# A two-layer trunk of four parallel mixers: layer 0 opens tile by tile of the channels over all eight PSUM banks

## The chip, the cores and the metric

One Trainium2 chip, one core of it. The metric is the device time of one execution in microseconds. The engines: TensorE (PE) multiplies matrices, VectorE (DVE), ScalarE (ACT) and GpSimd (POOL) do the elementwise work, SyncE (SP) issues most transfers. Each engine takes its instructions in the order in which the program gives them.

## What is computed

Two layers on 256 tokens of 1024 channels, all in float32. Each layer norms x, scales and shifts it by the conditioning c, multiplies it by one wide input matrix (7124 columns), sends the columns through four mixers, merges these by gates, projects, adds, and then runs a squared-ReLU MLP. Cut:

```python
for l in range(DEPTH):
    cmod = (c_act @ ada_w[l] + ada_b[l])[:, None, :]
    sh1, sc1, g1, sh2, sc2, g2 = jnp.split(cmod, 6, axis=-1)
    h = _rmsnorm(x, norm_mix_g[l]) * (1.0 + sc1) + sh1
    z = h @ w_in[l]
    za, zb, zc, zd, zg = _split(z, [A_COLS, B_COLS, C_COLS, D_COLS, G_COLS])
    ya = _conv_branch(za, ...)         # gate and value, convolution of 31 taps
    yb = _sparse_attn_branch(zb, ...)  # top 64 keys of an indexer, attention
    yc = _gla_branch(zc, ...)          # gated linear recurrence
    yd = _hgrn2_branch(zd, ...)        # gated linear recurrence
    gates = jax.nn.sigmoid(zg).reshape(B_, S_, N_BRANCH, D_)
    merged = jnp.sum(jnp.einsum('bsnw,nwd->bsnd', ys, w_branch_out[l]) * gates, axis=2)
    x = x + g1 * (merged @ w_o[l])
    h = _rmsnorm(x, norm_mlp_g[l]) * (1.0 + sc2) + sh2
    x = x + g2 * (jnp.square(jax.nn.relu(h @ mlp_w1[l])) @ mlp_w2[l])
return _rmsnorm(x, final_g)
```

## The kernel before

A product is made of float32r matmuls: each operand is split into a high and a low part, and three products (high by high, high by low, low by high) are accumulated in PSUM (`mm3`). A weight slab of up to 128 x 1024 is loaded by SP (`do_load`, line 412, pool `raw` of 5 places, and 8 more places for the first conditioning slabs), and split by ScalarE (high part `wh`) and VectorE (low part `wl`) in `do_split` (429). A conditioning slab isn't split: VectorE multiplies it by c and sums it along the row into one column (`use`, 650; a "sum" below).

The order of all instructions is written by the planner in the kernel. `items` are the steps of TensorE's main stream, each with the slabs it needs; `run` (453) goes through them, loads ahead as places come free, and splits ahead as far as `LOOK` (6500 ns of planned work) unless an item says otherwise. Smaller work lies in chains (generators): B0 and B1 (attention of the two token tiles), A (convolution), C and D (recurrences). `weave` (196) puts steps of chains between the matmuls where the planner's clocks (`note`, durations in `_Meter`) say that their inputs are there, and `drain` (208) emits a chain to its end, and of the others every step that would start earlier by those clocks, with a handicap of 300 ns plus the chain's `PRIO` (88: B 300, D 400, C 500, A 1000). In `_Meter` an affine_select of GpSimd is priced at 330 ns plus 10 ns a row of its innermost dimension, a memset or copy of 256 elements at 245 ns.

PSUM has eight banks: four (`mm`, taken by `mm_take`) serve the main stream, four are the mixers' working banks (`b2`, two pairs, 1035); in the opening of layer 0 the latter four hold the transposed x (`accs`).

The opening of layer 0 (`start`, 1564, and `layer`, 1596): SP loads the small inputs, c on all partitions (`crow`), two conditioning slabs and then x. `norm_first` (785) norms x, transposes it into the four `accs` banks, and, as each channel tile's scale and shift have been summed up, makes hT, the high and low part of that tile of h, from there. `early(k)` (1618) multiplies channel tile k by branch B's 724 columns (slabs b0, b1; tokens on partitions, four `mm` banks, 12 matmuls of 362 columns). The conditioning slabs come two of the scale and two of the shift at a time. `mask_consts` (990) makes seven masks for the recurrences on GpSimd in this stage, and `other_consts` (865) the tables of angles, bounds, selectors. After branch B, `change` (1666) opens the mixers' pools and spawns B0 and B1, and chunks of columns follow with the columns on partitions (`chan_chunk`, 561): ag and av (the convolution's gate and value), df and dq (D's forget and query factors), 48 matmuls of 256 columns each. Then di (with the tokens on partitions, 48 matmuls of 512 columns), cqk, cv, and the gates and projections of B, D, C, A in this order (`merge_items`, 1491), each of which drains its own chain first. The conditioning slabs for later parts are spread between these (`spread`, 379). In a level of `linear` (1283) two small products are followed by VectorE work and by a predicated copy that reads that level's mask.

Of the kernel before, what the change touches and what calls it, by code (L numbers as in the profile page):

```python
# [17 lines left out]
try:  # L18
# [15 lines left out]
P = 128  # L34
S = 256
# [38 lines left out]
# pieces of the input projection: columns, and how many k tiles a slab holds  # L74
WIN = {"b0": ([(512, 874)], 2), "b1": ([(874, 1220), (1988, 2004)], 2), "df": ([(2004, 2260)], 4),
       "dq": ([(2260, 2516)], 4), "di": ([(2516, 3028)], 2), "cqk": ([(1220, 1476)], 4),
       "cv": ([(1476, 1988)], 2), "av": ([(0, 256)], 4), "ag": ([(256, 512)], 4)}
for _i in range(8):
    WIN[f"g{_i}"] = ([(COL_G + 512 * _i, COL_G + 512 * _i + 512)], 2)
WIN_AT = {}  # L80
_off = 0
for _c, (_cols, _per) in WIN.items():
    _n = sum(b - a for a, b in _cols)
    WIN_AT[_c] = (_off, _n, _per)
    _off += _n * D
# [10 lines left out]
class Flow:  # L96
    """Emission order: a stream of weight slabs for the tensor engine, with chains of smaller work
    woven in between where a rough model of the engines says that their inputs are there."""
# [109 lines left out]
    def drain(self, ch, until=None):  # L208
        """emits a chain to its end (or until something holds), and what else can go on meanwhile"""
# [68 lines left out]
class _Pool:  # L278
    """a pool whose tiles are short-lived: the model knows when their places are free"""
# [15 lines left out]
class Slab:  # L295
    """A piece of a weight matrix: loaded, and split into two float32r parts when it says so."""
# [10 lines left out]
class Item:  # L307
    """A step of the tensor engine's main stream: the slabs it uses, what emits it, what comes before."""
# [8 lines left out]
def trunk_kernel(ctx, tc, x, c, cT, pos, chan, ada_w, ada_t, w_in, mlp_w1, gla_gate_w,  # L317
# [1668 lines left out]
```

## Time and profile before

| what | before |
| --- | --- |
| device time, median of 3 runs | 941.81 us (940.19 to 946.4) |
| span of the profiled execution | 943.6 us |
| TensorE busy in it | 897.3 us (95%) |
| VectorE busy | 713.9 us (76%) |
| ScalarE busy | 478.9 us (51%) |
| GpSimd busy | 110.4 us (12%) |
| read from memory | 194.97 MB, 208 GB/s over the span |

A busy engine is one that has an instruction in flight. A matmul's listed duration includes its way through the array, so neighbouring matmuls overlap; what one costs in a row of them is the distance between their starts. The granted clock is the share of full speed at which TensorE was allowed to run: 1.00 is 2.4 GHz, and 0.50 is 1.2 GHz.

### The profile page before, as it was taken

To read this page: it belongs to the slowest core of one execution; us is meant where nothing else is said; L and a number is where in the kernel's file an instruction comes from. 1 tells how busy PE (TensorE), PEld (TensorE's weight loads), DVE (VectorE), ACT (ScalarE), POOL (GpSimd) and SP (SyncE) were. 2 spreads that over 40 slices of the span, in tenths; PEclk is the share of its full clock that TensorE was granted. 3 is DMA by queue.
4 is the path that set the end of the run, shared out by engine and by line. 5 is a ranking of instruction groups with operands and counts; after the bars stand their busy time and mean duration, and the time that the engine had idled before them with its cause. 6 is when DMAs were issued, how large, how long until landed. Compare 5 with 4: busy or idle time off the path is not lost. (4 is left out here: it accounts for less than half of the span.)

```text
span 943.6 us, 14391 instructions
## 1 busy us (share of the span) xinstructions
PE 897.3 (95%) x5320; PEld 753.0 (80%) x5320; DVE 713.9 (76%) x1204; ACT 478.9 (51%) x787; POOL 110.4 (12%) x158
## 2 busy tenths in 40 slices
PE   1699999999999999999999999999999999999996
PEld 1699766767778899998978887777777889999995
DVE  7989788787767878888776988887876784555553
ACT  6474754324454544444575567333455564544451
POOL 6800010101000001111110001021000001111110
PEclk9899999999999999999999999999999999999998
DMA  8878545465644598999954554445655456666641
GB/s 315 307 253 284 188 152 179 163 194 179 230 144 158 194 312 322 316 316 315 323 192 174 168 180 155 137 151 158 223 166 172 153 183 221 225 210 216 219 158 46
DMA packets 55558, 196.96 MB, mean 209 GB/s; under 512 B 6432, under 2 KB 6848, under 8 KB 55488
## 3 DMA queue, kind: packets, MB, share of 16 engines
q1 hardware_dynamic: 55488, 196.04, 61.8%
q8 instruction: 42, 0.69, 0.3%
q14 instruction: 28, 0.23, 0.1%
HBM read 194.97 MB, written 1.05 MB: 208 GB/s over the span
## 5 line engine op out<-in xcount | busy, mean ns | idle before, releaser
L273 DVE TENSOR_TENSOR wl<-raw,wh 128x1024 fp32r<-128x1024 f32 (+1 forms) x276 | 329.3, 1219 | 64.7 <-ACT wh L273 63.5
L273 ACT ACTIVATE wh<-raw 128x1024 fp32r<-128x1024 f32 (+1 forms) x276 | 277.6, 1040 | 129.9 <-DMA raw<-in_mlp_w 73.5
L273 PE MATMUL mm<-wh,hTh 128*128 128x512 f32 (+1 forms) x384 | 155.0, 404 | 8.5 <-ACT wh L273 5.1
L273 PE MATMUL mm<-wl,hTh 128*128 128x512 f32 (+1 forms) x384 | 148.1, 386 | 5.5 <-DVE wl L273 5.4
L273 PE MATMUL mm<-wh,hTl 128*128 128x512 f32 (+1 forms) x384 | 147.7, 385 | 0.0
L273 PE MATMUL mm<-h2h,wl 128*128 128x256 f32 x416 | 117.2, 282 | 0.0
L273 PE MATMUL mm<-h2l,wh 128*128 128x256 f32 x416 | 117.2, 282 | 0.0
L273 PE MATMUL mm<-h2h,wh 128*128 128x256 f32 x416 | 117.1, 282 | 0.0
L273 PEld LDWEIGHTS mm<-wh,hTh 128*128 128x128 f32 x384 | 73.2, 191 | 37.2 <-issue 11.9
L273 PE MATMUL acc<-wh,uH 128*128 128x512 f32 x256 | 101.7, 397 | 0.0
L273 PE MATMUL acc<-wl,uH 128*128 128x512 f32 x256 | 101.2, 395 | 0.5 <-DVE wl L273 0.5
L273 PE MATMUL acc<-wh,uL 128*128 128x512 f32 x256 | 101.1, 395 | 0.1
L273 DVE SCALAR_TENSOR_TENSOR raw<-raw,crow 128x1024 f32<-128x1024 f32 x72 | 90.8, 1269 | 3.0 <-DMA raw<-in_ada_t 2.7
L273 PEld LDWEIGHTS mm<-wl,hTh 128*128 128x128 f32 x384 | 73.4, 191 | 17.0 <-DVE wl L273 6.6
L273 PEld LDWEIGHTS mm<-wh,hTl 128*128 128x128 f32 x384 | 73.3, 191 | 13.8 <-DVE hTl L273 0.3
L273 PEld LDWEIGHTS mm<-h2h,wh 128*128 128x128 f32 x416 | 78.3, 188 | 1.0
L273 PEld LDWEIGHTS mm<-h2l,wh 128*128 128x128 f32 x416 | 78.3, 188 | 1.1
L273 PEld LDWEIGHTS mm<-h2h,wl 128*128 128x128 f32 x416 | 78.3, 188 | 0.1
L273 PEld LDWEIGHTS acc<-wh,uL 128*128 128x128 f32 x256 | 48.2, 188 | 11.5 <-DVE uL L273 0.5
L273 PEld LDWEIGHTS acc<-wl,uH 128*128 128x128 f32 x256 | 48.2, 188 | 11.0 <-DVE wl L273 1.1
L273 PEld LDWEIGHTS acc<-wh,uH 128*128 128x128 f32 x256 | 48.2, 188 | 9.7
L273 DVE SCALAR_TENSOR_TENSOR ca<-U,chp,ca 128x256 f32<-128x256 f32 x120 | 53.3, 493 | 0.0
(532 smaller groups left out, 1452.7 us busy)
## 6 DMA issues: line engine op xcount, KB each, us to landing
raw<-in_mlp_w SPq DMA_DIRECT2D x128, 512.0 KB, 5.1
raw<-in_w_in SPq DMA_DIRECT2D x100, 512.0 KB, 4.2
raw<-in_ada_t SPq DMA_DIRECT2D x72, 512.0 KB, 5.5
raw<-in_ada_w SPq DMA_DIRECT2D x24, 512.0 KB, 4.2
raw<-in_w_branch_out SPq DMA_DIRECT2D x16, 512.0 KB, 4.2
raw<-in_w_o SPq DMA_DIRECT2D x16, 512.0 KB, 4.2
raw<-in_w_in SPq DMA_DIRECT2D x16, 362.0 KB, 4.3
x<-in_x SPq DMA_DIRECT2D x2, 512.0 KB, 7.6
```

What stands on the lines that cost most here:

```text
L273: return fn(*args, **kw)
```

## The change

- Layer 0's input columns are packed anew: per channel tile one slab o0 of branch B's 724 columns and one slab o1 of 1024 columns (ag, av, df, dq). Layer 1 keeps its packing.
- The opening runs channel tile by channel tile: load and sum the tile's scale and shift, split o0 and o1, make the tile of h, and multiply it by both slabs at once: 12 matmuls of 362 columns into the four `mm` banks, 24 of 256 columns into the four `accs` banks (two results of 256 columns to a bank). All eight banks hold running sums until tile 7 is done.
- x is loaded first, on SP's queue; c, positions and the per-channel parameters are loaded from ScalarE's queue. c is no longer loaded on all partitions, but spread by eight matmuls and two copies. x is normed (VectorE multiplies, ScalarE did before), transposed, and copied from PSUM to SBUF once (`xT`), so that the banks are free.
- After tile 7 one item, `opened`, spawns the masks, empties all eight banks, opens the mixers' pools, spawns B0, B1, A and D, and drains the masks. Then comes di, as before.
- The masks' scratch is bf16 in a place of its own. The small rows (gw, ngc, ngd) are loaded in `opened`. The sines are computed after tile 0.

```diff
-WIN = {"b0": ([(512, 874)], 2), "b1": ([(874, 1220), (1988, 2004)], 2), "df": ([(2004, 2260)], 4),
-       "dq": ([(2260, 2516)], 4), "di": ([(2516, 3028)], 2), "cqk": ([(1220, 1476)], 4),
-       "cv": ([(1476, 1988)], 2), "av": ([(0, 256)], 4), "ag": ([(256, 512)], 4)}
...
+    _REST[f"g{_i}"] = ([(COL_G + 512 * _i, COL_G + 512 * _i + 512)], 2)
+
+WIN = [{"o0": ([(512, 1220), (1988, 2004)], 1), "o1": ([(256, 512), (0, 256), (2004, 2516)], 1), **_REST},
+       {"b0": ([(512, 874)], 2), "b1": ([(874, 1220), (1988, 2004)], 2), "df": ([(2004, 2260)], 4),
+        "dq": ([(2260, 2516)], 4), "av": ([(0, 256)], 4), "ag": ([(256, 512)], 4), **_REST}]
...
+            junk = xTp.tile([P, D], BF16, name="junk1", tag="junk1")
+            A.activation(junk, xt[t], AF.Square, scale=1.0 / 32.0, accum_out=ss[:, 0:1])
+            G.tensor_scalar(ss[:, 0:1], ss[:, 0:1], EPS, None, op0=OP.add)
+            rs.append(rstd_of(ss[:, 0:1], 1))
+        for t in range(NT):
...
+                V.tensor_scalar(y, xt[t][:, c * 512:(c + 1) * 512], rs[t], None, op0=OP.mult)
+                pss[t, c] = bank(t, c)
                 for kk in range(4):
-                    T.transpose(pss[t, c][:, kk, :], y[:, kk * P:(kk + 1) * P], ident)
...
+    def tile_first(k, scale, shift, h):
+
+        scale.finish_on_act(k)
+        shift.finish_on_act(k)
+        tm = work.tile([P, 512], F32, name="hf", tag="t512", bufs=5)[:, 0:S]
+        A.activation(tm, state["xT"][:, k, :], AF.Identity, scale=scale.col[:, k:k + 1],
+                     bias=shift.col[:, k:k + 1])
+        A.activation(h[0][:, k, :], tm, AF.Copy)
+        V.tensor_tensor(h[1][:, k, :], tm, h[0][:, k, :].bitcast(F32), op=OP.subtract)
...
+        def angles():
+            for r in range(2):
+                A.activation(sin2[:, :, r, :], ang, AF.Sin)
+                A.activation(cos2[:, :, r, :], ang2, AF.Sin)
+        state["angles"] = angles
...
     def mask_consts():
-        while "rms" not in state:
-            fl.ctx.blocked = True
-            fl.ctx.t = fl.clock["pe"] + 300.0
-            yield
-        fl.ctx.blocked = False
         masks = consts.tile([P, 7, S], U8, name="masks")
-        mks = zp.tile([P, NT * 704 + 64], F32, name="mks", tag="Z")
+        mks = consts.tile([P, 2, S], BF16, name="mks")
...
         for lv in range(7):
-            yield
+            yield "pool"
...
+            mk = mks[:, lv % 2, :]
+            G.memset(mk, 1.0)
+            mv = mk.rearrange("p (r b i) -> p r b i", r=4, i=m)
...
-            G.tensor_copy(masks[:, lv, :], mk32)
...
+            G.tensor_copy(masks[:, lv, :], mk)
...
-        nc.sync.dma_start(ccol, cT)
-        nc.sync.dma_start(crow, bass.AP(tensor=c.tensor, offset=c.offset, ap=[[0, P], [1, D]]))
-        sp["t"] = 2000.0
...
+        nonlocal xTp
+        xTp = state["ctx"].enter_context(tc.tile_pool(name="xTp", bufs=1, side="right"))
+        nc.scalar.dma_start(ccol, cT)
+        nc.scalar.dma_start(posi, pos)
+        nc.scalar.dma_start(chp, chan)
+        for t in range(NT):
+            nc.sync.dma_start(xt[t], x[t * P:(t + 1) * P, :])
...
+        for _ in range(4):
             do_load(pos_of["load"])
...
+        A.activation(cg, ccol, AF.Sigmoid)
+        V.tensor_tensor(cs, ccol, cg, op=OP.mult)
+        G.tensor_copy(cb, cs[:, :, None].to_broadcast([P, KD, 32]))
+        pcs = mm_take(2)
+        for c in range(2):
+            for j in range(4):
+                k = 4 * c + j
+                T.matmul(pcs[c][:, j * P:(j + 1) * P], cs[:, k:k + 1].to_broadcast([P, P]), ident,
+                         start=True, stop=True)
+        other_consts()
+        V.tensor_copy(crow[:, 0:512], pcs[0])
+        pool = state["ctxp"].enter_context(tc.tile_pool(name="accs", bufs=1, space=PSUM))
+        state["bank"] = lambda t, c: pool.tile([P, 512], F32, name="accs", tag=f"accs{t}{c}")
+        state["xps"] = rows_first(state["bank"])
+        A.activation(crow[:, 512:1024], pcs[1], AF.Copy)
+        mm_free(*pcs)
+        state["xT"] = xTp.tile([P, KD, S], F32, name="xT", tag="xT")
+        transposed(0)
...
+            A.activation(state["xT"][:, 4 * c:4 * c + 4, t * P:(t + 1) * P],
+                         state["xps"][t, c].rearrange("p (k i) -> p k i", i=P), AF.Copy)
...
+            def early(k):
+                def f():
...
+                    if k == 0:
+                        tok.update({(part, t): mm_take(1)[0] for part in range(2) for t in range(NT)})
+                    s = so[0][k]
+                    for part, (c0, c1) in enumerate(cols_b):
+                        for t in range(NT):
+                            fl.weave()
+                            ts = slice(t * P, (t + 1) * P)
+                            mm3(tok[part, t][:, :c1 - c0], h[0][:, k, ts], h[1][:, k, ts], s.h[:, 0, c0:c1],
+                                s.l[:, 0, c0:c1], k == 0, k == KD - 1)
+                    s = so[1][k]
+                    if k == 0:
+                        banks_ = [state["bank"](t, c) for c in range(2) for t in range(NT)]
+                        chn.extend(banks_[m // 2][:, m % 2 * S:(m % 2 + 1) * S] for m in range(8))
+                    for m in range(8):
+                        cs = slice(m * P, (m + 1) * P)
+
+                        T.matmul(chn[m], s.h[:, 0, cs], h[0][:, k, :], start=k == 0 and m % 2 == 0, stop=False,
+                                 skip_group_check=True)
+                        T.matmul(chn[m], s.h[:, 0, cs], h[1][:, k, :], start=False, stop=False,
+                                 skip_group_check=True)
+                        T.matmul(chn[m], s.l[:, 0, cs], h[0][:, k, :], start=False, stop=k == KD - 1 and m % 2 == 1,
+                                 skip_group_check=True)
+                        fl.weave()
+                return f
...
+            at = len(items)
+            for k in range(KD):
+                add(lambda: None, [opening[0][k].need[0]], None, 0.0)
+                add(lambda: None, [opening[1][k].need[0]], None, 0.0)
+                add(lambda: None, [so[0][k]], None, 0.0)
+                if k == 0:
+                    add(first_tile(k), (), None, 0.0)
+                    add(lambda: None, [so[1][k]], None, 0.0)
+                    add(lambda: transposed(1), (), None, 0.0)
+                else:
+                    add(lambda: None, [so[1][k]], None, 0.0)
+                    add(first_tile(k), (), None, 0.0)
+                add(early(k), [so[0][k], so[1][k]], None, 4800.0)
+                if k == 0:
+                    add(lambda: state["angles"](), (), None, 0.0)
+            for it in items[at:-1]:
+                it.look = 0.0
...
+            def opened():
+                small_rows()
+                state["masks"] = fl.spawn("masks", mask_consts())
+                for part in range(2):
+                    for t in range(NT):
+                        mix.done_b(part)(t, tok[part, t][:, :362])
+                        mm_free(tok[part, t])
+                change()
+                mix.done_agate(chn[0:2])
+                mix.done_aval(chn[2:4])
+                mix.done_df(chn[4:6])
+                mix.done_dq(chn[6:8])
+                state["ctxp"].close()
+                mix.open_ps()
+                mix.start_b()
+                fl.drain(state["masks"])
+
+            at = len(items)
+            add(opened, (), None, 0.0)
+            items[at].closes = True
```

## Rows read from the trace of the kernel before

**Rows 1.** Page: busy us, share, instructions; TensorE's tenths in 40 slices.

```profile
PE 897.3 (95%) x5320; PEld 753.0 (80%) x5320; DVE 713.9 (76%) x1204; ACT 478.9 (51%) x787; POOL 110.4 (12%) x158
...
PE   1699999999999999999999999999999999999996
```

**Rows 2.** Stages: length, busy us (instructions) by engine, granted clock, DMA share, GB/s.

```profile
0.00:22.50 22.50, 3.94 (x16) 3.14 (x16) 16.18 (x49) 15.36 (x34) 14.24 (x48) 1.00 0.87 314
22.50:52.70 30.20, 20.73 (x96) 18.82 (x97) 27.81 (x36) 17.80 (x42) 20.48 (x23) 0.89 0.79 292
52.70:79.10 26.40, 26.40 (x222) 25.61 (x221) 24.88 (x57) 16.75 (x30) 0.15 (x1) 1.00 0.79 260
79.10:263.20 184.10, 182.84 (x990) 133.68 (x989) 148.87 (x283) 88.91 (x138) 14.46 (x13) 1.00 0.59 195
```

**Rows 3.** What TensorE waited for, whole span: total us, times, longest us.

```profile
PE accs L273 <- ACT ynorm L273: 16.0, 2, 14.5
PE mm L273 <- DVE wl L273: 6.9, 5, 2.6
```

**Rows 4.** TensorE's timeline: start, us, engine, line, operation, tiles, shapes, count.

```profile
25.07 0.51 PE L273 MATMUL mm<-wh,hTh 128*128 128x362 f32 x1
25.37 0.51 PE L273 MATMUL mm<-wl,hTh 128*128 128x362 f32 x1
...
28.16 0.33 PE L273 MATMUL mm<-wh,hTh 128*128 128x362 f32 x1
28.33 0.33 PE L273 MATMUL mm<-wl,hTh 128*128 128x362 f32 x1
...
52.73 0.28 PE L273 MATMUL mm<-hTh,wh 128*128 128x256 f32 x1
52.84 0.28 PE L273 MATMUL mm<-hTl,wh 128*128 128x256 f32 x1
...
79.14 0.40 PE L273 MATMUL mm<-wh,hTh 128*128 128x512 f32 x1
```

**Rows 5.** VectorE's timeline, opening and just after it.

```profile
14.69 1.22 DVE L273 SCALAR_TENSOR_TENSOR raw<-raw,crow 128x1024 f32<-128x1024 f32 x1
...
15.98 1.23 DVE L273 SCALAR_TENSOR_TENSOR raw<-raw,crow 128x1024 f32<-128x1024 f32 x1
...
54.79 2.36 DVE L273 TENSOR_TENSOR wl<-raw,wh 128x1024 fp32r<-128x1024 f32 x2
```

**Rows 6.** VectorE's groups by form: total us, mean ns; to 53 us, then 53 to 270.

```profile
L273 DVE SCALAR_TENSOR_TENSOR raw<-raw,crow 128x1024 f32<-128x1024 f32 x16 | 22.8, 1459 | 1.8 <-DMA raw<-in_ada_t 1.6
...
L273 DVE TENSOR_TENSOR wl<-raw,wh 128x724 fp32r<-128x724 f32 x8 | 9.6, 1243 | 0.1
...
L273 DVE SCALAR_TENSOR_TENSOR raw<-raw,crow 128x1024 f32<-128x1024 f32 x8 | 9.7, 1214 | 0.0
```

**Rows 7.** Transfers, 0 to 50 us: rate in 40 slices of 1.25 us.

```profile
GB/s 0 108 82 223 288 344 419 419 419 419 416 403 404 381 408 390 338 193 350 403 408 394 408 406 398 401 330 234 241 376 367 347 262 33 0 288 184 344 364 344
```

**Rows 8.** All engines' timeline, the first sum of a conditioning slab.

```profile
9.10 1.52 DVE L273 SCALAR_TENSOR_TENSOR raw<-raw,crow 128x1024 f32<-128x1024 f32 x1
```

**Rows 9.** ScalarE, first stage after branch B: a timeline line, a group by form.

```profile
55.72 1.28 ACT L273 ACT_TABLE_LOAD   x1
...
L273 ACT ACTIVATE U<-mm 128x256 f32<-128x256 f32 x2 | 0.8, 386 | 1.3 <-PE mm L273 1.3
```

**Rows 10.** VectorE's timeline, the end of B0's search and D's start.

```profile
100.50 0.28 DVE L273 SCALAR_TENSOR_TENSOR sc<-sc,nc 128x128 f32<-128x128 f32 x1
...
101.03 0.67 DVE L273 TENSOR_TENSOR qk<-Qd,Kd 128x512 f32<-128x512 f32 x1
```

**Rows 11.** GpSimd's timeline, the first and the last piece of the masks.

```profile
16.28 0.31 POOL L273 MEMSET mks<- 128x256 f32 x1
...
43.20 0.93 POOL L273 CAST masks<-mks 128x256 uint8<-128x256 f32 x1
```

More of the change, by code (lines that the diff above doesn't have):

```diff
@@ L807, in norm_first @@
-        state["there"] = state["allowed"] = 0
-        for k in range(KD):
-            while min(scale.summed, shift.summed, state["allowed"]) <= k:
-                fl.ctx.blocked = True
-                fl.ctx.t = fl.clock["pe"] + 200.0
-                yield
-            fl.ctx.blocked = False
-            yield "act"
-            scale.finish_on_act(k)
-            shift.finish_on_act(k)
-            tm = work.tile([P, 512], F32, name="hf", tag="t512", bufs=5)[:, 0:S]
-            for t in range(NT):
-                A.activation(tm[:, t * P:(t + 1) * P], pss[t, k // 4][:, k % 4, :], AF.Identity,
-                             scale=scale.col[:, k:k + 1], bias=shift.col[:, k:k + 1])
-            A.activation(h[0][:, k, :], tm, AF.Copy)
-            yield "dve"
-            V.tensor_tensor(h[1][:, k, :], tm, h[0][:, k, :].bitcast(F32), op=OP.subtract)
-            state["there"] = k + 1
+                    T.transpose(pss[t, c][:, kk * P:(kk + 1) * P], y[:, kk * P:(kk + 1) * P], ident)
@@ L951, in other_consts, with masks_and_selectors @@
         V.tensor_tensor(sc_, sc_, chp[:, 0, PC_G1:PC_G1 + 8], op=OP.mult)
-        sg = rows.tile([P, D], F32, name="row", tag="row")
-        cg = consts.tile([P, KD], F32, name="cg")
-        A.activation(cg, ccol, AF.Sigmoid)
-        A.activation(sg, crow, AF.Sigmoid)
-        V.tensor_tensor(crow, crow, sg, op=OP.mult)
-        G.tensor_tensor(cb, ccol[:, :, None].to_broadcast([P, KD, 32]),
-                        cg[:, :, None].to_broadcast([P, KD, 32]), op=OP.mult)
-        for r in range(2):
-            A.activation(sin2[:, :, r, :], ang, AF.Sin)
-            A.activation(cos2[:, :, r, :], ang2, AF.Sin)
+        def angles():
[3 more added lines that the diff above has]
+        state["angles"] = angles
+    def masks_and_selectors():
         onesd = consts.tile([P, P], F32, name="onesd")
@@ L1565, in start @@
         open_hl2()
[L1566 removed]
+        state["ctx"], state["ctxp"] = ExitStack(), ExitStack()
         raw0["pool"] = state["ctx"].enter_context(tc.tile_pool(name="raw0", bufs=NB_RAW0, side="right"))
[L1568 to L1573 removed]
+        nonlocal xTp
@@ L1584, in start @@
-        state["hT"] = new_hT("hT", actp)
-        state["norm"] = fl.spawn("norm", norm_first(first[1], first[0], state["hT"], state["bank"]))
-        state["masks"] = fl.spawn("masks", mask_consts())
+        cg = consts.tile([P, KD], F32, name="cg")
+        cs = consts.tile([P, KD], F32, name="cs")
+        A.activation(cg, ccol, AF.Sigmoid)
[7 more added lines that the diff above has]
+                         start=True, stop=True)
@@ L1666, in change @@
         def change():
-            fl.drain(state["masks"])
             state["ctx"].close()
@@ L1957, in _layout @@
     for l in range(depth):
-        for c, (cols, per) in WIN.items():
+        for c, (cols, per) in WIN[l].items():
             w = np.concatenate([a['w_in'][l][:, c0:c1] for c0, c1 in cols], axis=1)
```

153 lines of the change are left out of this document (50 added, 103 removed).

## The prediction, made before the changed kernel ran

> **What bounds the kernel now.** I read the page's busy shares and slices first, then busy time by stage, then what TensorE waits for, then the timelines of each engine in the opening. The shares: TensorE is busy 897.3 of 943.6 us, and its slices show the holes at the two ends only [rows 1]. So the kernel is bound by TensorE, and what can be won is idle time, 46.3 us of it. By stage [rows 2]: to 22.5 us TensorE works 3.9 us (18.6 idle), from there to the end of branch B's projection at 52.7 us it works 20.7 of 30.2 (9.5 idle), then it is full to 79.1 us. 28.1 of the 46.3 us lie in the opening. The waits name them: 16.0 us for the normalised x, and 6.9 us for split weights [rows 3]. Outside the opening the mixers (79.1 to 263.2 us) hide nearly everything: 1.3 us idle, with VectorE at 149 of 184 us [rows 2]. The time is therefore set by how early TensorE has a supply of work, and after that by its own work.
>
> **Prices.** From the starts of neighbouring matmuls: 362 columns take 0.30 us at 25 us and 0.165 us at 28 us (the half clock, 1.2 GHz, and the full one, 2.4 GHz), 256 columns 0.12 us [rows 4]. A sum of one conditioning slab on VectorE takes 1.29 us from start to start, a split of 1024 columns 1.18 us (two in 2.36) [rows 5]. These are prices with GpSimd quiet. Beside the masks the same sum takes 1.46 us on the mean against 1.21 afterwards, and a split of 724 columns 1.24 us [rows 6]; by its columns it should be 1.18 x 724/1024 = 0.83 us.
>
> **The opening, changed.** TensorE's work per channel tile is 12 matmuls of 362 columns and 24 of 256: 12 x 0.165 + 24 x 0.12 = 4.9 us. VectorE per tile: two sums (2.58), the splits of 724 and 1024 columns (0.83 + 1.18) and the low part of h (about 0.35): 4.9 us; with the masks' contention left in it would be 5.7. Transfers per tile: 0.524 x 3 + 0.371 = 1.94 MB; the slices of the queue's rate reach 400 to 419 GB/s where nothing holds them [rows 7], so 4.8 us. Three suppliers at one pace, so each tile costs about 4.9 us, and TensorE should have no hole beyond a few tenths between tiles.
>
> The start: the first sum begins at 9.10 us before [rows 8]. Now x is loaded ahead of it (1.05 MB, 2.6 us at 400 GB/s, but it is issued some 2 us earlier, since the small loads go to ScalarE's queue), c is spread over the partitions by eight matmuls instead of a load, and four multiplications of x by its row factor stand before the first sum in VectorE's queue. I take 9.7 us. Two sums, the 724-column split, the wait for ScalarE and hTl bring the first matmul to about 14 us; tile 0 runs partly at half clock, which is hidden because VectorE must deliver tile 1 in any case, at 9.7 + 2 x 4.9 + 0.7 = 20.2 us. Then six more tiles and the last one's own work: 20.2 + 7 x 4.9 = 54.5 us. Bounds: 52.5 us if the start is no later than before, 57.5 us if a tile costs 5.3 us (the masked price of the 724-column split).
>
> Before, the same work (branch B, and the ag, av, df, dq columns) is done at 79.14 us, where the columns di begin [rows 4]. In between TensorE also did branch B's first small products: 26.4 us less 192 x 0.12 and 2 x 0.165 is 3.0 us [rows 2, 4]. These come later now. Gross: 79.1 - 54.5 - 3.0 = 21.6 us. No matmul and no split is removed: the 16 weight slabs of this work (eight of 724 columns, eight of 1024) are only cut anew. The rest of the edits is hidden: the eight matmuls that spread c run while TensorE has nothing else; ScalarE, busy 17.8 us in 30.2 for about six tiles [rows 2], 3.0 each, gets one split more per tile (about 1.0) and one activation less, some 3.6 of 4.9 us; the four copies of the transposed x and the sines with their table load fall into tile 0, where TensorE waits for VectorE. If that cover is gone they cost tile 0 about 2 us once.
>
> **What the end of the opening gives back.** The change spawns the masks only after the last tile and drains them before the first di matmul is issued. In the planner's own prices the seven masks take 6.3, 3.7, 2.4, 1.8, 1.5, 1.3 and 1.2 us, so about 18 us of the other chains' steps (B0, B1, D, A) are put into the queues ahead of di. TensorE executes in order: di waits behind the last chain product emitted in that stretch, though its weights are split. Behind that wait stands the whole stream; nothing else fills TensorE.
>
> How late is that last product? Let 0 be the end of the opening. ScalarE empties eight banks (a table load of 1.28 us and some 5 us of copies and sigmoids, from -2.9 us on, when the B banks are complete) [rows 9], so to about 3; VectorE follows with the gates at about 3.3, ropes 2.6 us, B's first products and D's first level are on TensorE by about 10. Then both top-8 searches hold VectorE, and D, whose priority is lower, starves: before, D's first product of Q and K came at 101.03, directly after the mask operation of B0's search at 100.50 [rows 10]. So D's second level and B0's second product come at 17 to 19, at the edge of the stretch. If they fall outside it, di starts at about 10.5, of which TensorE has used 4.4 (3.0 for B, 1.4 for D's sums and first level); it then has about three split slabs (8.1 us), and waits for the fourth until VectorE has worked off the chain steps ahead of its split, at about 21: lost 21 - 8.1 - 4.4 = 8.5 us. If they fall inside, di starts at 18.5 with 5.5 us used: lost 13 us. To either add the ramp after a nearly idle stretch: before, nine matmuls ran at 0.30 instead of 0.165 us [rows 4], 1.2 us. I take the first, with the ramp: 10 us. Bounds: 3 us (a short stretch, almost all used), and 18 us (masks at the chip's pace, below).
>
> The masks themselves cost VectorE as they did before: on the chip they took GpSimd from 16.28 to 44.1 us [rows 11], 28 us against the planner's 18. At 1.46/1.21 VectorE loses up to 5 us of 28; D needs mask 0 first, at 6, which comes in time. The VectorE work moved behind the opening (chain work and the gate's sums, about 16 us) is mostly done in the lost 10 us, so I carry nothing on: VectorE has 35 us of slack to 263 us [rows 2]. The small bias and row loads now stand behind the slabs on SP's queue and are first needed by the di evacuation; hidden.
>
> **Sum.** 943.6 - 21.6 + 10 = 932.0 us for a profiled execution. The median of the runs, 941.81 us, is 1.8 us below the profiled one, so 930 us.
>
> **Rivals.**
> 1. The drain costs its whole length: B0's and D's products fall inside the stretch, 14 to 18 us lost. For it: TensorE is strictly in order and the stretch is 18 us in the planner's prices. Against it: D starves. 943.6 - 21.6 + 16 - 1.8 = 936 us.
> 2. The drain is nearly free: the last product comes early and the split of the fourth slab is not behind it; 3 us lost, 923 us. Against it: VectorE's queue has some 17 us of chain steps by then.
> 3. The loads don't keep 400 GB/s: at the mean of the old opening, 314 and 292 GB/s [rows 2], a tile takes 6.2 to 6.6 us, and the opening ends about 10 us later: 940 us. Against it: those means hold stretches in which buffers weren't free [rows 7].
> 4. Slower: TensorE stays at the half clock through the opening. Before, with bursts of 24 matmuls and waits between, the granted clock was 0.89 of full in that stage [rows 2], and the burst at 25 us began at 0.30 us [rows 4]. At that level a tile costs 12 x 0.30 + 24 x 0.22 = 8.9 us (0.22 scaled by 0.30/0.165), 4.0 us more, 32 us in eight tiles: 962 us. It decides from three tiles on (the 11.6 us net are gone) and is over 1% slower from six. Against it: the gaps between tiles should be tenths. The Trainium skill ("TensorE: Matmul & The Clock Gate", the section on HAM oscillation) describes a loop that waits for its loads between k tiles and falls back to the cold clock in every one; the burst at 25 us agrees.
> 5. GpSimd shuts VectorE out. Beside the masks one sum took 1.46 instead of 1.21 us, a partial slowing [rows 6]; were it full, the chains' two-input steps would stand still for most of the masks' 28 us, and D, B0 and di's later splits with them: 20 us or so lost instead of 10, 940 us. The Trainium skill ("SBUF — State Buffer", the section on the two separate sides) calls the pair shared by both engines an exclusive lock for a whole instruction; by it this rival holds, by the row the 5 us above do, and the trace so far shows the smaller.
>
> **How the numbers follow.** Forecast 0.42 (926 to 934), rival 1 0.22, rival 2 0.11, rival 3 0.08, rival 4 0.06, rival 5 0.06; 0.05 for a slower order of the chains later (the planner's clocks shift, B's end is already drained for). A measurement of this kernel tells about 1% from no change, that is 932.4 and 951.2 us. Faster: most of the forecast and rival 2, 0.48. Slower: rival 4 and most of the last, 0.10. The rest, 0.42. The range takes rivals 1, 2, 3 and 5 at their edges: 922 to 942 us.
>
> **What would show it.** The di columns begin near 65 us (73 in rival 1); per tile TensorE's starts repeat every 4.9 us from 20 us on, with the granted clock at 1.0; a hole in TensorE with only small products of B and D right after the last tile; sums at 1.21 us in the opening. I am wrong if the tiles come every 6 us or more, if the clock falls in the opening, or if D or A is late at its own projection and gives back time there.

## The result: slower, and the profile after

| what | before | after |
| --- | --- | --- |
| device time, median | 941.46 us (940.19 to 946.4, 4 runs) | 988.4 us (985.68 to 990.4, 4 runs) |
| span of the profiled execution | 943.6 us | 988.7 us |
| mean granted clock of TensorE in it | 0.992 | 0.957 |

The ratio after to before is 1.0484, with an interval of 1.0453 to 1.0515: 4.8% slower, where 1.2% faster was forecast.

The page of the changed kernel (busy times; then 40 slices of 24.7 us: TensorE, its granted clock, the DMA share, the rate):

```profile
span 988.7 us, 14426 instructions
...
PE 915.4 (93%) x5336; PEld 767.7 (78%) x5336; DVE 713.1 (72%) x1209; ACT 476.1 (48%) x774; POOL 110.1 (11%) x158
...
PE   5999964299999999999999999999999999999996
...
PEclk9999955599999999999999999999999999999998
DMA  8967700045674559899985454545454547665651
GB/s 342 366 215 236 262 32 0 0 149 160 224 242 159 173 173 327 316 319 335 324 305 186 155 173 150 171 127 191 151 177 146 188 146 259 225 222 193 201 182 43
```

The opening is as full as it was meant to be: the first slice of TensorE is 5 and the next four are 9, against 1, 6, 9, 9, 9 [rows 1]. But the sixth to the eighth slice (about 124 to 198 us), 6, 4 and 2, hold a hole that the kernel before does not have. The rate there falls to 32, 0 and 0 GB/s, so no slab is loaded ahead either, and the granted clock is 5 tenths, the lower of its two levels (1.2 GHz).

Busy time by stage of the changed kernel (from, to; length; busy us and instructions of each engine; granted clock, DMA share, GB/s):

```profile
19.40:60.50 41.10, 40.85 (x288) 40.38 (x289) 38.27 (x57) 31.16 (x61) 0.00 (x0) 1.00 0.93 342
60.50:122.40 61.90, 59.18 (x298) 46.01 (x297) 56.82 (x118) 38.57 (x62) 30.52 (x33) 1.00 0.68 226
122.40:198.30 75.90, 34.72 (x201) 27.24 (x200) 51.02 (x118) 18.03 (x44) 6.89 (x6) 0.53 0.05 16
198.30:323.30 125.00, 122.97 (x584) 86.56 (x585) 70.28 (x100) 47.32 (x59) 3.95 (x3) 0.99 0.57 188
```

What TensorE waited for in the changed kernel, the largest (total, times, longest):

```profile
PE b L276 <- DVE ca L276: 18.4, 1, 18.4
PE b L276 <- POOL Fd L276: 5.9, 2, 5.0
PE b L276 <- DVE Qd L276: 5.4, 3, 2.3
```

Of the two waits of [rows 3], the 16.0 us for the normalised x are 3.7 and the 6.9 us for split weights are 2.8. The three above are new and all of `b`, the working banks of the chains; the longest is for branch A's `ca`, the convolution that VectorE works out tap by tap.

**Where the time went**, stretch by stage of the profiled executions. Before: di starts at 79.14 us, branch B's projection at 149.63, the last matmul of A's projection at 279.67, the end at 943.6. After: 60.55, 198.34, 323.25, 988.7. So the opening gave 18.6 us; from di to B's projection it took 137.8 us instead of 70.5, a loss of 67.3; from there to A's last matmul 124.9 instead of 130.0, 5.1 less, since chain work was already done; the rest is 1.5 us longer. Sum: 67.3 + 1.5 - 18.6 - 5.1 = 45.1 us, the difference of the two spans.

The instructions at the two ends of the hole, changed kernel. VectorE's timeline: B0's rotations, the end of B0's softmax, the last low part of D, the last taps of A, the last low part of A:

```profile
75.31 0.68 DVE L276 TENSOR_TENSOR ra<-Z,cos 128x160 f32<-128x160 f32 x1
...
128.26 0.69 DVE L276 TENSOR_TENSOR M<-M,rs 128x512 f32<-128x512 f32 x1
...
167.97 0.42 DVE L276 TENSOR_TENSOR yslD<-b,yshD 128x256 fp32r<-128x256 f32 x1
168.31 16.71 DVE L276 SCALAR_TENSOR_TENSOR ca<-U,chp,ca 128x256 f32<-128x256 f32 x42
...
196.23 0.69 DVE L276 TENSOR_TENSOR yslA<-ca,yshA 128x512 fp32r<-128x512 f32 x1 [0.70 <-ACT yshA L276]
```

and TensorE's timeline: the transposes of that same softmax, and B's projection:

```profile
192.23 1.06 PE L276 MATMUL b<-ident,M 128*128 128x128 f32 x4
...
198.34 0.80 PE L276 MATMUL mm<-wh,yshB 128*128 128x512 f32 x1 [0.48 <-ACT yshB L276]
```

M is ready at 129 us and transposed at 192, after D has ended and A's last product has been made. TensorE takes its instructions in order, so it is the order that the planner wrote down. It comes from these lines of `Flow.drain`, the loop that emits a chain to its end:

```python
go = [c for c in self.chains if not c.blocked] or self.chains
self.step(min(go, key=lambda c: self.start(c) + (0.0 if c is ch else 300.0 + PRIO...)))
```

A chain that asks for a pair of working banks while both are taken is marked `blocked`, and the mark is only lifted when the chain itself is tried again. Here that means: when no unblocked chain is left. In the planner's run the drain of B0 makes ten steps; the tenth is B0's request for its transposes, which finds both pairs held (by D and B1) and marks the chain. Then come 88 steps of other chains (A 42, D 29, B1 11, C 6) before B0 is tried once more, though the pairs are given back many times in between. In the kernel before B0 has ended by then, and what is drained is B1, which is never marked.

### The profile page after: what moved, and what is told of

The parts are those of the page before. It is cut to its first block, busy times and chain, and to the rows that moved or that the text cites. A ratio compares the mean times of both kernels' runs of the same rounds, so it can differ in the third digit from the quotient of the medians.

```text
span 988.7 us, 14426 instructions
## 1 busy us (share of the span) xinstructions
PE 915.4 (93%) x5336; PEld 767.7 (78%) x5336; DVE 713.1 (72%) x1209; ACT 476.1 (48%) x774; POOL 110.1 (11%) x158
## 5 line engine op out<-in xcount | busy, mean ns | idle before, releaser
L276 DVE SCALAR_TENSOR_TENSOR raw<-raw,crow 128x1024 f32<-128x1024 f32 x72 | 88.1, 1231 | 0.3 <-DMA raw<-in_ada_t 0.3
L276 PEld LDWEIGHTS mm<-wh,hTl 128*128 128x128 f32 x384 | 72.7, 189 | 14.2 <-DVE hTl L276 0.9
```

The lines of the kernel that those rows point to most:

```text
L276: return fn(*args, **kw)
```

## The experiments

**Theory 1:** this order makes the hole. **Rivals:** M, the masks (now behind the opening) slow VectorE and make the chains late; C, the half clock in the hole is its cause. **Theory 2**, for what is left once theory 1 had been tested: B's chains start too late to be done when the stream needs them. Its rival is V: VectorE is full, and any order gives the time back.

### Trying blocked chains again, in both kernels

```diff
 def free(self, t_):
     self.b2s[self.b2_of.pop(t_.tensor.name)] = fl.last(t_.tensor.name) + 50.0
+    for c_ in fl.chains:
+        c_.blocked = False
```

The changed kernel with it:

> The changed kernel with one rule of its planner altered: when a pair of PSUM banks is given back, every chain that was marked as blocked is tried again. Theory 1 (an order): a chain that finds both pairs taken is marked blocked and passed over as long as any other chain can go on, so at branch B's projection D and A are emitted to their very ends ahead of B0's last transposes, and TensorE, in order, waits from 122.4 to 198.3 us. Then the projection of B begins when the chains B0 and B1 are done, between 131 us (70.5 us after di's start at 60.55, the distance in the kernel before) and 147 us (where B1's last step ran here anyway), not at 198.3; time 988.4 less 51 to 67 = 921 to 937 us, and I take 935, since B0's ropes start at 75.3 us all the same. Rival M (the masks, moved behind the opening, slow VectorE and make the chains late): the hole stays in its main part, over 975 us. Rival C (the half clock in the hole is the cause): the chain products run at half clock as before, over 965 us.

947.05 us median (943.39 to 953.73), ratio to before 1.0044 [1.0017, 1.0072]. By stage:

```profile
60.50:122.50 62.00, 59.71 (x309) 47.32 (x309) 57.22 (x118) 38.04 (x64) 30.06 (x33) 1.00 0.67 227
122.50:146.70 24.20, 16.04 (x100) 10.90 (x98) 17.53 (x37) 10.65 (x26) 2.01 (x2) 0.57 0.16 62
```

and TensorE's timeline at B0's transposes and at B's projection:

```profile
132.34 1.09 PE L276 MATMUL b<-ident,M 128*128 128x128 f32 x4 [1.40 <-DVE big L276]
...
146.75 0.80 PE L276 MATMUL mm<-wh,yshB 128*128 128x512 f32 x1
```

Two lines of the planner give back 41 us of the 47. The transposes now follow M, ready at 130.02 us, within 2.3 us, and the hole ends at 146.75 us, at the upper end of what was expected. The time missed its range by 10 us: the stretch behind B's projection takes longer again, since D and A still have to be done there (146.75 to A's last matmul at 282.06 is 135.3 us, after 124.9). Against the kernel before, by the same stretches as above: di starts 17.1 us earlier (62.06), 14.2 of these are lost from there to B's projection (84.7 instead of 70.5 us), where 24 us with little stream work remain, with the clock at 0.57, and 5.3 from there to A's last matmul. So the whole gain of the opening is gone again.

The kernel before with it:

> The kernel before with the same altered rule. Theory 1: its chains were not passed over at branch B's projection (B0 was finished, B1 went on), so nothing to gain: within 0.5% of the kernel before, 938 to 945 us. If the altered rule were a gain in itself, and not the cure of what the change brought, it would be under 930.

943.21 us, ratio 0.9997 [0.998, 1.0014]. The rule is no gain in itself.

### Putting the masks back, and forcing the order in the kernel before

```diff
         masks_and_selectors()
+        fl.drain(fl.spawn("masks", mask_consts()))
...
-                state["masks"] = fl.spawn("masks", mask_consts())
...
-                fl.drain(state["masks"])
```

> The changed kernel with only the masks put back: emitted to their end in the opening, right after the selectors, none of them behind it; the rule for blocked chains as in the changed kernel. Theory 1: B0 still finds both pairs taken at the projection of B, so the hole stays: B's projection at 190 to 200 us, 980 to 995 us (the opening loses up to 5 us to the masks beside VectorE, the chains behind it win 3). Rival M: the chains come in time, under 950 us.

989.5 us, ratio 1.0486 [1.0454, 1.0517]. The opening's stage:

```profile
19.40:60.50 41.10, 36.48 (x250) 34.92 (x251) 41.06 (x51) 27.11 (x52) 27.15 (x27) 0.92 0.82 290
```

and TensorE's timeline at di's start and at B0's transposes:

```profile
66.41 0.50 PE L276 MATMUL mm<-wh,hTh 128*128 128x512 f32 x1 [0.63 <-ACT Z L276]
...
193.79 1.06 PE L276 MATMUL b<-ident,M 128*128 128x128 f32 x4
```

Rival M falls: without any mask behind the opening the transposes still come at 193.8 us. The opening pays 4 to 6 us for the masks (di at 66.4 instead of 60.55, and of 60.8 to 62.1 in the other runs with this opening), VectorE being busy for all of those 41 us.

```diff
-add(proj(t), sl, (lambda nm=nm: self.finish(nm)) if t == 0 else None, 2600.0)
+add(proj(t), sl, (lambda nm=nm: self.finish("DAB" if nm == "B" and l == 0 else nm)) if t == 0 else None, 2600.0)
```

(`finish` takes the branches letter by letter.)

> The kernel before with one order forced: at branch B's projection in layer 0 the chains D and A are emitted to their ends first, and then B. Old opening, masks in the opening, TensorE's stream as before. Theory 1: this order by itself makes the hole: the projection of B moves from 149.6 us to 185 to 195 us, with TensorE at half clock in between, and the time rises by 33 to 48 us, to 975 to 990. Rivals M and C, for which the new opening or the masks' place is needed: within 10 us of the kernel before.

983.76 us, ratio 1.0425 [1.0393, 1.0457]. The stage of the hole:

```profile
150.00:186.00 36.00, 11.00 (x68) 9.52 (x68) 25.21 (x62) 1.96 (x4) 3.43 (x3) 0.55 0.00 0
```

and TensorE's timeline at A's first product and B's projection:

```profile
188.81 2.05 PE L273 MATMUL b<-ca,onesd 128*128 128x256 f32 x4 [19.71 <-DVE ca L273]
...
196.12 0.77 PE L273 MATMUL mm<-wh,yshB 128*128 128x512 f32 x1
```

The old opening with the masks in their old place shows the same hole, the same wait for `ca`, no transfers and a clock of 0.55, as soon as D and A stand ahead of B: 40 us for an order. So the half clock follows from the hole and is not its cause; rival C falls with M. How much of the hole the lower level adds was not separated: in the changed kernel TensorE is busy 34.72 of its 75.90 us, so it is at most half of the 34.72, 17 us (an estimate).

### What is left: B's chains are late

```diff
 (the rule for blocked chains altered, and the masks put back as above)
```

> The changed kernel with the altered rule for blocked chains, and the masks put back into the opening: against the run with the altered rule alone (947.05 us) this prices the masks' place. The opening will end near 66 us instead of 61 (as in the run with the masks early and the old rule), and VectorE, no longer slowed by the masks behind the opening, wins that time back for the chains of B. Theory 2 (what is left of the hole at B's projection, 122.8 to 146.8 us, comes from B's chains, which start at 76 us and share a VectorE that is 57.2 of 62 us busy): B's projection begins at 141 to 149 us, and the time stays within 5 us of 947. Rival M (the masks behind the opening are what makes the chains late): B's projection before 138 us and 940 us or less.

947.42 us, ratio 1.0049 [1.0023, 1.0074]. di starts at 66.73 us, B's projection at 147.28. The masks' place is worth nothing either way: what the opening saves without them, the chains behind it lose with them.

```diff
                 change()
+                mix.start_b()
+                for t in range(NT):
+                    for _ in range(2):
+                        fl.step(mix.chain[f"B{t}"])
                 mix.done_agate(chn[0:2])
...
-                mix.start_b()
```

> The changed kernel with the altered rule, and the rotations of B0 and B1 put into VectorE's queue directly after B's columns are copied out, ahead of the gates' work of A and D (two more buffers for the doubled keys). Theory 2: the start of B's chains sets the end of the hole; the rotations run at 62 to 66 us and not at 76 to 84, B's projection begins 6 to 10 us earlier, at 137 to 141 us, and the time falls to 937 to 942. Rival V (VectorE is full until the searches are done, so that an earlier start only displaces other work of it): B's projection at 144 us or later, 944 to 948 us.

953.46 us, ratio 1.0096 [1.0062, 1.013]: worse, and for a reason that neither theory named. VectorE's and TensorE's timelines:

```profile
61.05 0.33 DVE L276 TENSOR_TENSOR ra<-Z,cos 128x160 f32<-128x160 f32 x1 [0.83 <-PE accs L276]
...
72.02 0.42 DVE L276 TENSOR_TENSOR Qd<-accs,Qd 128x256 f32<-128x256 f32 x1 [0.45 <-ACT Qd L276]
...
72.59 1.09 PE L276 MATMUL b<-ident,Z 128*128 128x128 f32 x4 [8.87 <-DVE Qd L276]
```

The rotations did come 15 us earlier. B0's transposes were therefore emitted earlier too, right behind two k tiles of di; but their banks are those of the opening's results, and VectorE empties the last of them only at 72.4 us. TensorE stood 8.87 us at its in-order head. B's projection came at 149.23, 2.5 us later than with the altered rule alone; in the end the run is 6.4 us later, and what the other 3.9 are is open. This run therefore says nothing on whether an earlier start of B's chains would have helped.

```diff
-        spread(at + 1, [it for v in PLAN["mixers", l] for it in vecs[v].fill()])
+        spread(at + 1 + (18 if l == 0 else 0), [it for v in PLAN["mixers", l] for it in vecs[v].fill()])
```

> The changed kernel with the altered rule, and the conditioning slabs of layer 0's mixers spread from the end of B's gates on instead of from di's second slab on, so that VectorE has six sums of 1.2 us less, 7.5 us, between 60 and 122 us. If B's chains are late because VectorE is full there (57.2 of 62 us), B's projection comes 4 to 8 us earlier, at 139 to 143 us, and the time falls to 940 to 945 (some of it is paid behind, where the slabs now stand closer). If it is the length of their own chain of dependent steps from 76 us on, B's projection stays at 146 to 147 and the time at 946 to 950.

957.74 us, ratio 1.0157 [1.0129, 1.0184]. B0's search ended at 105.07 us instead of 116.86 and B's projection began at 141.89, 4.9 earlier (1.3 of these because di began at 60.78 and not at 62.06), as rival V's first half says: VectorE's load sets when B ends. The time was a miss by 13 us. By stage, up to B's projection and from there to A's last matmul:

```profile
122.50:141.90 19.40, 12.01 (x85) 8.28 (x83) 14.93 (x32) 6.37 (x16) 2.04 (x2) 0.69 0.21 83
141.89:292.74 150.85, 141.30 (x697) 99.33 (x696) 111.17 (x194) 55.95 (x77) 7.75 (x7) 0.94 0.58 189
```

and the latter stretch in the run with the altered rule alone:

```profile
146.75:282.06 135.31, 133.40 (x690) 95.25 (x688) 102.93 (x182) 55.06 (x76) 8.88 (x7) 0.99 0.52 175
```

The lead of 4.9 us turns into 10.7 us behind, because this stretch takes 15.5 us more. TensorE is idle 9.6 us in it instead of 1.9, with six sums of conditioning slabs on VectorE before D's projection, where the other run has none. And by the mean clock it spends some 18 us at the lower level instead of some 3; half of these 15 us, with the 7.6 us more of idle time, is nearly the whole difference (an estimate).

### Work for TensorE that waits for no chain

```diff
 # layer 0: columns g (gates) of B, g of D, and then the projections of B and D
+late = [(proj, sl, nm)]
+if l == 0 and i < AHEAD:            # AHEAD = 1
+    held.append((proj, sl, nm)); late = []
 for c in range(2):
     tok_chunk(h, gsl[c], done(c))
+if l == 0 and i == AHEAD:
+    late = held + late
...                                 (the projections in late follow, in this order)
```

With the altered rule:

> The changed kernel with the altered rule, and in layer 0 the gate columns of D ahead of B's projection (21 us of work for TensorE that waits for no chain). Theory 2: the hole is filled; B's projection begins at 146 to 152 us without a hole of over 3 us ahead of it; D's projection follows it directly, near 160 us, where D is not ready (in the run with the altered rule alone its projection began at 196.5), so a second hole of 5 to 15 us comes there; 930 to 942 us. Rival V (VectorE is full): the splits of the gate columns delay B's searches by as much, the hole only moves, and the time is 944 us or more.

933.52 us, ratio 0.9889 [0.9854, 0.9924]. With the rule as it was:

> The changed kernel with the gate columns of D ahead of B's projection in layer 0, and the rule for blocked chains left as it was. Theory 1 says that a blocked chain is passed over only while another chain is drained; with 21 us more of TensorE's stream ahead of B's projection the chains of B end by themselves, and nothing is left to drain. Then this is as good as the run with both edits: 931 to 937 us, B's projection near 176 us with TensorE full before it. If the pass-over also acts outside a drain, or the altered rule was what gained, a hole stays before B's projection: over 945 us.

932.86 us, ratio 0.9881 [0.9859, 0.9903]. By stage, of the latter:

```profile
60.50:122.50 62.00, 58.87 (x292) 46.76 (x291) 58.07 (x123) 38.19 (x68) 26.38 (x33) 0.94 0.68 223
122.50:147.00 24.50, 22.42 (x158) 15.72 (x160) 22.45 (x44) 15.96 (x38) 1.90 (x2) 1.00 0.40 130
147.00:198.00 51.00, 50.90 (x304) 35.33 (x303) 45.51 (x90) 19.31 (x25) 3.79 (x3) 1.00 0.54 171
```

B's projection begins at 177.30 us in it. There is no hole before it, and the clock is 1.00 from 122.5 us on (the 0.94 ahead of that is some 7 us at the lower level from 72 us on, behind a wait of 1.9 us for split weights). The drain that made the hole finds B0 and B1 done, so the rule doesn't matter, and rival V falls: this order doesn't give the time back. The second hole that I expected before D's projection didn't come either (D's projection runs at 185.3 us in the latter). Is it the gate columns' place alone? The kernel before with the same order:

> The kernel before, with the gate columns of D ahead of B's projection in layer 0. It separates what the gate columns' place is worth by itself from what it gives the changed kernel. Before, TensorE had 1.3 us idle from 79 to 263 us, so there is nothing for this order to fill: 940 to 946 us, ratio within 0.4% of 1. Then the 10 us that the changed kernel with this order is faster are the new opening's. If the order is a gain of its own, this runs at 933 to 937 us, and the new opening is worth next to nothing even here.

946.89 us, ratio 1.0038 [1.0019, 1.0057]: slightly slower, 0.9 us over the range expected. So the order gains only with the new opening: 932.86 us with it, 946.89 without.

### The start

```diff
-        both = [bounds(), rotations()]
-        ...                             (both, step by step in turn)
+        for _ in rotations():
+            pass
 def angles():
+    for _ in bounds():
+        pass
```

> The changed kernel with the altered rule, and the bounds of the forget gate moved from the start to the sines in tile 0, so that ScalarE's sum of squares does not stand behind an exponential that waits for the parameters until 8.8 us, and VectorE's factor for the rows of x can come earlier. The first sum of a conditioning slab then begins near 11.5 us instead of 13.8, the first matmul near 17.5 instead of 19.4, and the opening ends 1.5 to 2.5 us earlier. If the time behind the opening is set by VectorE and B's chains, these move along by as much: 944.5 to 946 us; if the bounds' work only moves into tile 0 and holds that up, no gain: 947.

946.46 us against 947.05 with the altered rule alone: no difference that can be told. The first sum came at 12.64 us and not near 11.5, tile 0's first matmul at 17.92 instead of 19.42. But the exponential and its table load now stood beside the sines' in tile 0: TensorE waited 1.44 us for tile 1, which came at 25.89 after 26.75, then ran matmuls of 362 columns 0.30 us apart again, and tile 2 came at 32.91, after 31.60 in the changed kernel. di began at 61.86 us, so nothing was left of it there. With the sines moved to the end of tile 7 as well, on top of the gate columns' place and the altered rule:

> The changed kernel with the altered rule, the gate columns of D ahead of B's projection, the bounds of the forget gate taken out of the start, and the sines with them moved from tile 0 to the end of tile 7, where ScalarE was idle (54.4 to 57.5 us). Tile 0 then starts near 17.9 us as in the run with the start alone, tile 1 no longer waits for ScalarE's table loads (20.35 to 22.1 us in the changed kernel) and starts near 23 us, and the opening ends at 57 to 58 us instead of 60.5. Behind it TensorE's stream is nearly full (7 us idle from 60 to 280), so the gain stays: 929 to 932 us against 933.5. If VectorE is behind in 60 to 122 us and gives the gain back, 933 us.

932.2 us, ratio 0.9878 [0.9858, 0.9899]. Tile 0 at 16.95, tile 1 at 24.59 (not near 23: TensorE worked through tile 0 without a wait, its first twelve matmuls 0.30 us apart), di at 59.23 us; of the 2.1 us that di is earlier than without these two edits (61.29), 1.7 are left at A's last matmul (268.12 against 269.80), but the ratios of the three kernels with this order, 0.9878, 0.9881 and 0.9889, lie within each other's intervals; the changed kernel with only the gate columns moved is the simplest that beats both kernels, by 1.2% the one before.

## Why the prediction was wrong, step by step

**The tiles: right.** "Each tile costs about 4.9 us": tiles 1 to 4 start at 26.75, 31.60, 36.39 and 41.20 us, 4.8 apart, and TensorE is busy 40.85 of 41.10 us. Rivals 3 (slow loads) and 4 (half clock through the opening) fall here. Tile 0 alone ran in part at the lower level, which the row's mean clock of 1.00 doesn't show; see the next point. The sums take 1.22 us in this stretch, as expected without masks beside them.

**The start: 6 us too early.** VectorE's and TensorE's timelines in the changed kernel:

```profile
7.91 0.17 DVE L276 COPY mxl<-chp 128x2 f32<-128x2 f32 x1 [2.78 <-DMA chp<-in_chan]
...
11.44 0.68 DVE L276 COPY crow<-mm 128x512 f32<-128x512 f32 x1
12.04 1.81 DVE L276 TENSOR_SCALAR ynorm<-x,rstd 128x512 f32<-128x512 f32 x4
13.77 1.21 DVE L276 SCALAR_TENSOR_TENSOR raw<-raw,crow 128x1024 f32<-128x1024 f32 x1
...
19.42 0.67 PE L276 MATMUL mm<-wh,hTh 128*128 128x362 f32 x1 [3.01 <-ACT hTh L276]
...
22.89 0.50 PE L276 MATMUL mm<-wh,hTh 128*128 128x362 f32 x1
23.19 0.50 PE L276 MATMUL mm<-wl,hTh 128*128 128x362 f32 x1
...
26.75 0.33 PE L276 MATMUL mm<-wh,hTh 128*128 128x362 f32 x1
```

I put the first sum at 9.7 us and it came at 13.77. Ahead of it in VectorE's queue stand the four multiplications of x, and ahead of these the small instructions of the bounds and the angles and a copy of c. They begin when the load of the per-channel parameters lands, at 7.9 us, and from there VectorE has no wait of over 0.04 us up to the first sum. The row factors are not what it waits for: GpSimd has them at 11.04 and 12.20 us, the multiplications that use them begin at 12.04 and 12.98. I had counted the four multiplications and not the queue in front of them. Taking the bounds out of it brought the first matmul to 17.92 us. The other 2 us are tile 0 itself. I had said that it runs partly at half clock and that this is hidden, because VectorE delivers tile 1 only at 20.2 us. It isn't hidden: the first twelve matmuls of tile 0 stand 0.30 us and more apart, the distance at 1.2 GHz [rows 4], TensorE has no wait of over 0.23 us in the tile, and it takes 7.33 us instead of 4.9. VectorE and ScalarE had tile 1's first operands ready at 25.4 us, before TensorE came to it at 26.75. The sines' table load, which I had named as a possible 2 us, is hidden behind that: with the sines moved away, tile 1 still came 7.64 us after tile 0. Opening's end: 60.55, not 54.5, outside my bounds of 52.5 to 57.5. Gross gain by the same sum: 79.1 - 60.55 - 3.0 = 15.6 us, not 21.6.

**The drain of the masks: 10 us too dear.** di starts 0.12 us after the last matmul of the opening (60.43), and no chain product stands ahead of it. I had taken the masks' 18 us for a stretch in which the other chains are emitted too. But `drain` always picks the step that can start first, and GpSimd had idled from 16.6 us on, so in the planner's count every step of the masks could start long before any chain's; it emitted the eight steps of the masks and nothing else. Rival 2 was right on this point. A drain is free where the drained chain is early, and dear where it is late, or marked. At di's start the two errors partly cancel, by luck: 15.6 us are won there where the sum had 21.6 - 10 = 11.6, and di begins at 60.55 us, not near 65. So the whole miss lies behind di's start, 60.7 us of it where the prediction carried nothing (988.7 - 943.6 + 15.6).

**The masks beside VectorE: a lock for some instructions, a slowing for others.** GpSimd's and VectorE's timelines, changed kernel:

```profile
61.24 4.31 POOL L276 TENSOR_SCALAR_AFFINE_SELECT mks<-mks 128x256 bf16<-128x256 bf16 x2
...
66.34 2.60 POOL L276 TENSOR_SCALAR_AFFINE_SELECT mks<-mks 128x256 bf16<-128x256 bf16 x2
...
62.02 0.76 DVE L276 TENSOR_TENSOR U<-accs,U 128x256 f32<-128x256 f32 x2 [2.16 <-ACT U L276]
...
63.43 2.26 DVE L276 TENSOR_SCALAR Kd<-Kd,oml 128x256 f32<-128x256 f32 x1
...
66.33 1.42 DVE L276 TENSOR_SCALAR Kd<-Kd,oml 128x256 f32<-128x256 f32 x1
```

That Kd instruction takes 0.35 us with GpSimd quiet (in the kernel before, and in the run with the masks back in the opening); here it ends at 65.69 us, just as GpSimd's second select ends at 65.55, and the next one, of 1.42 us, ends with the select beside it. The two `U<-accs,U`, each with one of its two inputs in PSUM, take 0.76 us beside the first select, as they do with the masks back in the opening. The splits, with two inputs, rose from 1.22 to 1.33 us on the mean of the 17 between 60.5 and 122.4 us. The Trainium skill ("SBUF — State Buffer", the section on the two separate sides) calls the port pair that the two engines share an exclusive lock for a whole instruction; the Kd row agrees with it. The splits, which by the same section the lock would hold up as well, agree only in part: one that begins at 72.31 us, beside a select that ends at 73.13, takes 1.74 us, 0.52 more than alone and not 0.82. Rival 5 nevertheless didn't decide the time: the masks in the opening or behind it gave 947.42 and 947.05 us.

**"Nothing carried on": the step that failed.** I wrote that VectorE has 35 us of slack up to 263 us and that B's end is already drained for, and gave a slower order of the chains 0.05. Both halves were wrong.

- The slack was a mean over 184 us [rows 2]. In the kernel before B0's search, from its rotations (57.06 us) to its last step (100.50), already ran on a full VectorE, 40.98 of 43.4 us; after, from 75.31 to the same step at 115.80, it is 40.23 of 40.5. The search takes 43.4 and 40.5 us, on a VectorE that the splits share and that is full in both (the two rows stand below). But before it began 22.1 us ahead of di's start, in the shadow of the columns ag to dq; after, 14.8 us behind it. The stream from di to B's projection is some 62 us of TensorE work (60.5 to 122.4), and with the order put right B ends at 147. This lateness then takes the opening's gain: 947.05 us. That the same amount of work moves behind the opening I had said ("about 16 us"), but not that it stands on the path to the next thing the stream waits for.

  The stretch of B0's search, in the kernel before:

```profile
57.10:100.50 43.40, 43.40 (x301) 39.31 (x301) 40.98 (x100) 23.95 (x37) 1.44 (x2) 1.00 0.83 274
```

  and in the changed one:

```profile
75.30:115.80 40.50, 39.45 (x207) 31.43 (x206) 40.23 (x94) 24.18 (x33) 16.68 (x19) 1.00 0.76 252
```

- "Drained for" is the contrary of safe. The drain is where a late chain stops the whole stream, its loads too, and the mark on blocked chains turned that into 76 us. By the runs: 988.4 with the mark, 947.05 with it lifted, 932.86 where the chains end before they are drained.

So of 988.4 - 932.9 = 55.5 us, 41 are the mark, and 14 are what the gate columns' place gives back on top, which I put down to the lateness of B's chains. The corrected sum without both would have been 943.6 - 15.6 - 1.8 = 926 us; the best three kernels stand at 932 to 934, and from 60.5 to 280 us TensorE is idle 7.0 us in the one with the gate columns moved (busy 212.50 of 219.50), which is about that difference.

**My own signs.** I had said that I would be wrong "if D or A is late at its own projection". It was B that was late, and D and A that were early at its expense.

## What to carry to other kernels

When work is pulled together at the front, ask of every chain that used to run in its shadow when it now starts, how long it runs beside everything else on its engine, and what the stream has to do until it is needed; slack is to be read in that stretch, not over the stage. Where a static order emits a chain "to its end", find out what else it emits first and whether a chain that once had to wait is ever looked at again. If the chain can't be earlier, put work that depends on nothing ahead of its use: moving 21 us of gate columns turned +4.8% into -1.2%, while earlier rotations, a lighter VectorE and a shorter start did nothing or worse.

## What the runs showed of the hardware

- TensorE's granted clock is 1.00 in the 62 us before the hole, in which it was busy 59.18 us, and 0.53 on the mean in it (34.72 of 75.90 us busy, the work there itself stretched by the lower level); 0.55 in the forced order's hole (11.00 of 36.00 us busy), 0.57 in the smaller one with the rule altered (16.04 of 24.20). It comes with a sparse TensorE in either opening, and is back at 0.99 in the stretch after.
- One VectorE instruction of 128 x 256 with one tensor input stood still for a whole GpSimd select (half of the 4.31 us of two): 2.26 us instead of 0.35; the next one took 1.42. Two instructions of the same size with one of their inputs in PSUM lost nothing beside a select (0.76 us for both), and two-input instructions of four times the size lost about a tenth on the mean of that stage (1.33 us instead of 1.22).
